# Two blocks on one core: experts' sums in pairs, the overflow loop inside a condition, and a ninth 2 MB slot for weights

## The chip, the cores and the metric

The kernel runs on one core of a Trainium2 chip. The time is the device time of one execution in microseconds (us). Of the core's engines, TensorE (PE in the profile) multiplies matrices, with weight loads (PEld) beside it; VectorE (DVE), ScalarE (ACT) and GpSimd (POOL) work on elements; SyncE (SP) only issues transfers from HBM, which 16 DMA engines carry out. SBUF is the memory on the chip, PSUM the memory into which TensorE writes.

## The reference

A token block of 256 x 1024 in float32 goes through two layers of a network. The first layer has a mixer, a layer norm and 32 experts of which each token takes 4; the second has another mixer and a gated MLP. The change lies in the first layer's norm and experts:

```python
h = layer_norm(DEEPNORM_ALPHA * h + mix, ln1_g[l], ln1_b[l])
ffn = moe(h, router_w[l], router_b[l], expert_w_up[l], expert_b_up[l], expert_w_down[l], expert_b_down[l])
h = layer_norm(DEEPNORM_ALPHA * h + ffn, ln2_g[l], ln2_b[l])

# moe, for each block of slots of one expert e:
hcat = xblk @ w_up[e] + b_up[e]                 # 1024 -> 2048
x_glu = minimum(hcat[:, 0::2], 7.0)
x_lin = clip(hcat[:, 1::2], -7.0, 7.0)
act = x_glu * sigmoid(1.702 * x_glu) * (x_lin + 1.0)
y = act @ w_down[e] + b_down[e]                 # 1024 -> 1024
# and for each token: the sum over its four experts of gate * y
```

One expert has 8.39 MB of up weights and 4.19 MB of down weights, 32 experts 402.7 MB, and each byte is read once. They come in chunks of 2.097 MB (2048 KB), called 2 MB here.

## The kernel before

The program is one long list of instructions for each engine, written out in Python; the order on each engine is the order of the code. It has three stages: the mixer of the first layer, the experts, and the second layer.

**Slots of an expert.** Each expert has 64 slots (`CAP`), to which the router's picks bring its tokens. `gather_group` (line 1079 issues its matmuls) brings the tokens of four experts at a time into `xt`, transposed, by matmuls with 0/1 matrices. An expert with more than 64 tokens puts the rest into an overflow table.

**One expert on TensorE.** `up` streams four chunks of 2 MB (two k-rows of 128 x 2048 each) and multiplies them with the expert's tokens (`up_k`, line 1027, 16 records a chunk), into `pu`. Inputs and outputs of 512 columns are laid as two halves of 64 partitions: 64 slots x two halves are 128 rows of PSUM. `swiglu` makes the activation on VectorE and ScalarE. `down` streams two chunks of 2 MB (`down_h`, line 1036, 16 records a chunk), and `out_copy` (line 1056) brings the result to SBUF as `y`, with columns 0 to 511 on partitions 0 to 63 and columns 512 to 1023 on partitions 64 to 127.

**Between the chunks.** The stages of several experts interlock. While expert e's up chunks run, behind the first of them, `between(1)` issues: the transposes of the activation of e-1 (`act_t`, line 1018), the sum of expert e-2's output into the tokens (`combine`, line 1066: four matmuls with 64 rows in, the gates at slots `gpt` as the stationary operand, and VectorE's addition of each to the tokens, line 1068), and the gates at slots for expert e (`gates_at_slots`: two picks on VectorE, line 1045, two transposes, line 1048, one copy). Then come the remaining three up chunks, and the down chunks of e-1. The last expert's down projection (`last_down`, lines 1161 and 1172) takes four pieces of 1 MB, so that the next norm's statistics can begin early. The last 2 MB chunk before the pieces is the second down chunk of expert 30.

**The ring of slots.** All weights come through `fetch` (line 129): it takes the oldest slot of a ring in SBUF and issues one transfer on SyncE's queue. A fetch into a slot waits until the engine that read it last is done. In the expert stage there are 8 slots of 2 MB: two in the arena `ring`, one in `ring1`, three in `ring2`, two in `lp`. They are filled ahead before the first expert starts, `lp` last, as its memory is in use until then.

**The middle.** After expert 15, and its two trailing sums, the number of overflow blocks is loaded into registers (line 1239), `lp` leaves the ring, six chunks are fetched ahead into the others, and a loop `For_i(0, n_over)` (line 1252) does the overflow blocks, with `lp` for their weights. Here the number is zero and the loop's body doesn't run; the loop's entry and exit synchronize all engines. Then `lp` joins the ring again, and experts 16 to 31 follow.

**The norm before the experts.** `route` normalizes the rows. Scale and shift (`ln1_g`, `ln1_b`) are folded into the weights of the router and the gathered tokens; for the residual path two rows are broadcast over 128 partitions by DMA, and GpSimd multiplies and adds them (`rest`). `gates` then scales by ALPHA and adds the gates times `b_down` (lines 931 and 933).

## Time and profile before

| | us |
|---|---|
| median of 3 runs (lowest, highest) | 1768.74 (1766.86, 1769.26) |
| the profiled execution | 1768.8 |
| its span, first to last instruction | 1767.0 |
| TensorE busy in it | 1656.0 (94%) |
| VectorE, ScalarE, GpSimd busy | 746.9, 556.8, 112.5 |
| bytes moved by DMA | 535.61 MB, 303 GB/s in the mean |
| mean granted clock of TensorE | 0.979 of full speed |

The profile is of one execution. Line numbers (L1027) are those of the program above. "Busy" of TensorE counts matmuls in the pipeline. Times in the views are counted from the start of the span. A group `pu<-ring,xt` says which tile is written and which are read. A wait is idle time of an engine just before an instruction, put down to what released it last. [...] The DMA share is the mean busy share of the 16 DMA engines; it can come out a little over 1.

### The profile page before, as it was taken

How to read it: one execution, taken by the hardware profiler on the slowest of the kernel's cores; microseconds unless marked ns; L12 is line 12 of the kernel's file. 1: busy time of each engine (PE TensorE's matmuls, PEld its weight loads, DVE VectorE, ACT ScalarE, POOL GpSimd, SP SyncE). 2: the span in 40 equal slices, each digit the busy share in tenths (PEclk: the TensorE clock that was granted, in tenths of full speed). 3: DMA queues.
4: the chain of work that ended last, by engine and by line, in shares of the span. 5: the costliest groups of instructions: out<-in, count | busy, mean ns of one | idle time of the engine just before them, and what ended most of it. 6: DMA issues, size and time to landing. Idle time of an engine off the chain costs nothing.

```text
span 1767.0 us, 23938 instructions
## 1 busy us (share of the span) xinstructions
PE 1656.0 (94%) x10141; PEld 1069.0 (60%) x10141; DVE 746.9 (42%) x1184; ACT 556.8 (32%) x859; POOL 112.5 (6%) x98
## 2 busy tenths in 40 slices
PE   8999989999999999799999999998999999999998
PEld 7999863333333333333333333347999999998997
DVE  5855542212222221122221222127677777566565
ACT  5446521110100100101001001015666556455444
POOL 5311220000000000000000000001211100000000
PEclk9999989999999999899999999998999999999999
DMA  9450979999999999899999999984554456455552
GB/s 314 134 165 1 351 287 427 404 407 427 427 427 427 426 428 427 359 418 427 427 428 428 426 428 427 427 313 157 174 168 139 148 168 207 164 167 191 191 187 76
DMA packets 149934, 535.61 MB, mean 303 GB/s; under 512 B 7123, under 2 KB 119139, under 8 KB 125504
## 3 DMA queue, kind: packets, MB, share of 16 engines
q1 hardware_dynamic: 147488, 529.68, 76.3%
q0 software_dynamic: 2048, 4.23, 0.8%
q8 instruction: 81, 1.33, 0.3%
q14 instruction: 29, 0.24, 0.0%
q10 hardware_dynamic: 288, 0.13, 0.0%
HBM read 532.97 MB, written 1.05 MB: 302 GB/s over the span
## 4 chain that ended last, share of the span: by engine, by line
PE 52%; DVE 4%; ACT 2%; issue 1%; DVEq 0%; ACTq 0%
PE pu L1027 13%; PE pj L163 8%; PE pj L165 7%; PE pj L164 7%; PE pd L1036 6%; PE pc L1066 2%; PE pa L164 1%; PE pa L163 1%; PE pa L165 1%; DVE xs L1068 1%; PE pc L1079 1%; DVE wl L158 1%; PE pu L1134 1%; PE px L1018 1%; PE po L1523 1%
## 5 line engine op out<-in xcount | busy, mean ns | idle before, releaser
L1027 PE MATMUL pu<-ring,xt 128*64 128x512 f32 x1600 | 369.2, 611 | 2.4 <-ACT xt L61 2.4
L158 DVE TENSOR_TENSOR wl<-ring,wh 128x1024 fp32r<-128x1024 f32 (+1 forms) x232 | 277.3, 1218 | 39.7 <-ACT wh L61 39.5
L61 ACT ACTIVATE wh<-ring 128x1024 fp32r<-128x1024 f32 (+1 forms) x247 | 252.3, 1029 | 85.8 <-PE pj L164 44.0
L1027 PEld LDWEIGHTS pu<-ring,xt 128*64 128x64 f32 x1600 | 111.5, 140 | 218.0 <-issue 209.7
L1068 DVE TENSOR_TENSOR xs<-xs,pc 128x512 f32<-128x512 f32 x124 | 79.7, 684 | 333.2 <-PE pc L1066 333.2
L1005 DVE TENSOR_SCALAR xg<-pu 128x512 f32<-128x512 f32 x32 | 22.1, 691 | 361.3 <-PE pu L1027 361.3
L165 PE MATMUL pj<-uth,wl 128*128 128x256 f32 x584 | 163.7, 280 | 4.4 <-DVE wl L158 4.4
L163 PE MATMUL pj<-uth,wh 128*128 128x256 f32 x584 | 165.7, 284 | 0.0
L164 PE MATMUL pj<-utl,wh 128*128 128x256 f32 x584 | 163.3, 280 | 0.0
L1036 PE MATMUL pd<-ring,act 128*64 128x512 f32 x704 | 154.8, 592 | 0.0
L61 ACT ACTIVATE sg<-xg 128x512 f32<-128x512 f32 x32 | 20.1, 630 | 334.9 <-DVE xg L1005 334.9
L165 PEld LDWEIGHTS pj<-uth,wl 128*128 128x128 f32 x584 | 110.5, 189 | 5.2 <-DVE wl L158 5.2
L163 PEld LDWEIGHTS pj<-uth,wh 128*128 128x128 f32 x584 | 110.8, 190 | 2.2 <-issue 2.1
L1066 PE MATMUL pc<-y,gpt 64*128 64x512 f32 x248 | 88.3, 641 | 24.9 <-DVE xs L1068 24.0
L1036 PEld LDWEIGHTS pd<-ring,act 128*64 128x64 f32 x704 | 50.5, 137 | 100.6 <-issue 100.6
L164 PEld LDWEIGHTS pj<-utl,wh 128*128 128x128 f32 x584 | 110.9, 190 | 0.1
L158 POOL TENSOR_TENSOR wl<-ring,wh 128x1024 fp32r<-128x1024 f32 x14 | 38.7, 2767 | 1093.2 <-PE pj L164 963.4
L1027 PE MATMUL pu<-lp,xt 128*64 128x512 f32 x448 | 104.2, 615 | 0.0
L163 PE MATMUL pj<-yah,wh 128*128 128x256 f32 x352 | 99.0, 281 | 0.0
L165 PE MATMUL pj<-yah,wl 128*128 128x256 f32 x352 | 98.9, 281 | 0.0
L164 PE MATMUL pj<-yal,wh 128*128 128x256 f32 x352 | 98.8, 281 | 0.0
L163 PE MATMUL pj<-xth,wh 128*128 128x256 f32 x288 | 83.1, 289 | 2.8 <-ACT wh L61 2.8
(441 smaller groups left out, 2808.6 us busy)
## 6 DMA issues: line engine op xcount, KB each, us to landing
ring<-in_expert_w_up_dram SPq DMA_DIRECT2D x100, 2048.0 KB, 18.8
ring<-in_expert_w_down_dram SPq DMA_DIRECT2D x44, 2048.0 KB, 16.4
ring<-in_w_in_dram SPq DMA_DIRECT2D x62, 1024.0 KB, 5.3
lp<-in_expert_w_up_dram SPq DMA_DIRECT2D x28, 2048.0 KB, 16.7
lp<-in_expert_w_down_dram SPq DMA_DIRECT2D x18, 2048.0 KB, 16.8
ring<-in_w_up_dram SPq DMA_DIRECT2D x22, 1024.0 KB, 5.0
ring<-in_w_down_dram SPq DMA_DIRECT2D x11, 1024.0 KB, 4.7
ring<-in_w_s_out_dram SPq DMA_DIRECT2D x8, 1024.0 KB, 4.8
```

Of the source, the lines that this page charges most:

```text
L61: self.nc.scalar.activation(out, x, func, **kw)
L158: return (hi_t, lo_t), lambda: (engine or g.nc.vector).tensor_sub(lo_t, src, hi_t)
L163: nc.tensor.matmul(out, a[0][asl], b[0][bsl], start=first, stop=False, skip_group_check=True)
L164: nc.tensor.matmul(out, a[0][asl], b[1][bsl], start=False, stop=False, skip_group_check=True)
L165: nc.tensor.matmul(out, a[1][asl], b[0][bsl], start=False, stop=last, skip_group_check=True)
L1005: nc.vector.tensor_scalar(xg, pv[:, :, 0], 7.0, None, op0=OP.min)
L1018: g.nc.tensor.transpose(pt[:, k], xv[:, k], g.ident)
L1027: g.nc.tensor.matmul(pu[hf * 64:hf * 64 + 64, b], x, ch[:, hf * D + b * 512:hf * D + b * 512 + 512], start=first, stop=last, skip_group_ch ...
L1036: g.nc.tensor.matmul(pd[n * 64:n * 64 + 64], act[:, k, hf], ch[:, s:s + 512], start=hf + k == 0, stop=hf * 4 + k == 7, skip_group_check=True)
L1066: nc.tensor.matmul(pc, gpt[s, tt], y[s], start=True, stop=True)
L1068: nc.vector.tensor_add(o, o, pc)
L1079: g.nc.tensor.matmul(pt[:, j], part[:, tt, (k + j) * P:(k + j + 1) * P], onehot(tt), start=tt + i == 0, stop=tt + i == 2)
```

## The change

- **A ninth slot.** The arena `ring2` gets 8 units instead of 6, so four slots of 2 MB instead of three; the ring of the expert stage has nine. Nine chunks are fetched before expert 0, and seven ahead of the loop. The memory comes from smaller scratch: the iota of 128 columns becomes one of 64, some tiles have one buffer instead of two, one tile of `swiglu` goes, and the scratch of GpSimd's DMA descriptors is 8192 instead of 16384 bytes.
- **Sums in pairs.** For an even expert e, `between(1)` issues the transposes alone; for an odd one it issues the sum of experts e-3 and e-2 together (`combine_pair`), and the gates at slots of experts e-1 and e (`pair_gates`). To put two experts' outputs on 128 partitions, `down` of an odd expert writes its column halves to the exchanged partitions, and two half copies on ScalarE lay the pair into one tile. Experts 30 and 31 are summed singly.
- **The condition.** The overflow loop stands inside `If(n_over > 0)`, and its loads are issued by GpSimd instead of SyncE.
- **Norm factors by products.** The broadcasts by DMA and GpSimd's four operations go. `gates`, now within experts 1 and 2, lets TensorE spread the scale over the partitions (eight matmuls with the identity), VectorE multiplies it into the tokens, and the shift comes in as a 33rd row of the product with `b_down`.
- **Swiglu.** The product with the sigmoid comes first, then the linear half.

```diff
@@ -36,7 +36,7 @@
 MANUAL = True
-RING, RING1, RING2 = 4, 2, 6
+RING, RING1, RING2 = 4, 2, 8
...
@@ -851,9 +852,7 @@
     n = len(g.ahead)
-    g.ahead += [fetch(g, *src) for src in (up_src(A, 0) + up_src(A, 1))[n:n + 2]]
-    ln = p.tile([P, 2, D], F32, name="ln")
-    gam, bet = bcast_row(g, ln[:, 0], "ln1_g"), bcast_row(g, ln[:, 1], "ln1_b")
+    g.ahead += [fetch(g, *src) for src in (up_src(A, 0) + up_src(A, 1) + down_src(A, 0))[n:n + 2]]
...
@@ -898,11 +897,7 @@
-    def rest():
-        for tt in range(2):
-            nc.gpsimd.tensor_mul(h[:, tt], h[:, tt], gam)
-            nc.gpsimd.tensor_add(h[:, tt], h[:, tt], bet)
-    return parts(), rest
+    return parts()
...
@@ -918,20 +913,31 @@
+    for n in range(2):
+        s = slice(n * 512, n * 512 + 512)
+        pt = pc_.tile([P, 512], F32, name="pc")
+        for k in range(4):
+            nc.tensor.matmul(pt[:, k * P:k * P + P], r.gb[:, 4 * n + k:4 * n + k + 1].to_broadcast([P, P]), g.ident,
+                             start=True, stop=True)
+        for tt in range(2):
+            nc.vector.scalar_tensor_tensor(h[:, tt, s], h[:, tt, s], ALPHA, pt, op0=OP.mult, op1=OP.mult)
+        yield
     pg = px.tile([NE, 2, P], F32, name="px")
     for tt in range(2):
         nc.tensor.transpose(pg[:, tt], r.gate[:, tt], g.ident)
-    nc.scalar.copy(gT, pg.rearrange("p a b -> p (a b)"))
+    nc.scalar.copy(gT[:NE], pg.rearrange("p a b -> p (a b)"))
     yield
     for tt in range(2):
         for n in range(2):
             pt = pc_.tile([P, 512], F32, name="pc")
             nc.tensor.matmul(pt, gT[:, tt * P:tt * P + P], r.bd[:, n * 512:n * 512 + 512], start=True, stop=True)
             s = slice(n * 512, n * 512 + 512)
-            nc.vector.scalar_tensor_tensor(h[:, tt, s], h[:, tt, s], ALPHA, pt, op0=OP.mult, op1=OP.add)
-    yield
+            nc.vector.tensor_add(h[:, tt, s], h[:, tt, s], pt)
+        yield
...
@@ -1000,13 +1006,12 @@
     xg = wp.tile([P, 512], F32, name="xg", bufs=1)
-    xl = wp.tile([P, 512], F32, name="xl", bufs=1)
     sg = wp.tile([P, 512], F32, name="sg", bufs=1)
     nc.vector.tensor_scalar(xg, pv[:, :, 0], 7.0, None, op0=OP.min)
     g.act(sg, xg, AF.Sigmoid, scale=1.702)
-    nc.vector.tensor_scalar(xl, pv[:, :, 1], 7.0, -7.0, op0=OP.min, op1=OP.max)
-    nc.vector.scalar_tensor_tensor(xg, xl, 1.0, xg, op0=OP.add, op1=OP.mult)
     nc.vector.tensor_mul(xg, xg, sg)
+    nc.vector.tensor_scalar(sg, pv[:, :, 1], 7.0, -7.0, op0=OP.min, op1=OP.max)
+    nc.vector.scalar_tensor_tensor(xg, sg, 1.0, xg, op0=OP.add, op1=OP.mult)
...
@@ -1028,26 +1033,52 @@
-def down_h(g, pd, act, ch, hf):
+def down_h(g, pd, act, ch, hf, swap=0):
     for k in range(4):
         for n in range(2):
             s = k * D + n * 512
-            g.nc.tensor.matmul(pd[n * 64:n * 64 + 64], act[:, k, hf], ch[:, s:s + 512],
+            m = (n ^ swap) * 64
+            g.nc.tensor.matmul(pd[m:m + 64], act[:, k, hf], ch[:, s:s + 512],
                                start=hf + k == 0, stop=hf * 4 + k == 7, skip_group_check=True)
...
@@ -1028,26 +1033,52 @@
+def pair_gates(g, r, wp, px, e, both=True):
+
+
+    nc = g.nc
+    gp = wp.tile([P, 2, 4, CAP], F32, name="gp", bufs=1)
+    for tt in range(2):
+        for i in range(2):
+            at = (slice(0, 3, 2) if i == 0 else slice(1, 2)) if both else slice(2 * i, 2 * i + 2)
+            n = 1 if both and i else 2
+            nc.vector.tensor_scalar(gp[:, tt, at], r.iota[:, None, :].to_broadcast([P, n, CAP]),
+                                    r.pos[:, tt, e + i:e + i + 1], r.gate[:, tt, e + i:e + i + 1],
+                                    op0=OP.is_equal, op1=OP.mult)
+    pt = px.tile([P, 2, 2, P], F32, name="px")
+    for i in range(2):
+        a = i if both else 2 * i
+        for tt in range(2):
+            nc.tensor.transpose(pt[:, i, tt], gp[:, tt, a:a + 2].rearrange("p a s -> p (a s)"), g.ident)
+    gpt = wp.tile([P, 2, 2, P], F32, name="gpt", bufs=1)
+    nc.scalar.copy(gpt.rearrange("p i t s -> p (i t s)"), pt.rearrange("p i t s -> p (i t s)"))
     return gpt
...
@@ -1064,6 +1095,17 @@
+def combine_pair(g, acc, pc_, y, gpt):
+
+    nc = g.nc
+    for tt in range(2):
+        for n in range(2):
+            pc = pc_.tile([P, 512], F32, name="pc")
+            nc.tensor.matmul(pc, gpt[:, n, tt], y[:, n], start=True, stop=True)
             o = acc[:, tt, n * 512:n * 512 + 512]
             nc.vector.tensor_add(o, o, pc)
...
@@ -1146,7 +1188,7 @@
         def at_slots(e):
-            gpt[e] = gates_at_slots(g, r, wp, px, lambda tt: r.pos[:, tt, e:e + 1], lambda tt: r.gate[:, tt, e:e + 1])
+            gpt[e] = pair_gates(g, r, wp, px, e, e < NE - 2)
...
@@ -1179,8 +1221,15 @@
             for hf, src in enumerate(down_src(A, e)):
-                down_h(g, pd, act[e], stream(g, *src), hf)
-            y[e] = out_copy(g, wp, pd)
+                down_h(g, pd, act[e], stream(g, *src), hf, e % 2)
+            if e == NE - 2:
+                y[e] = out_copy(g, wp, pd)
+                return
+            if e % 2 == 0:
+                y[e] = wp.tile([P, 2, 512], F32, name="y", bufs=1)
+            for i in range(2):
+                s = slice(i * 64, i * 64 + 64)
+                nc.scalar.copy(y[e - e % 2][s, i ^ (e % 2)], pd[s])
...
@@ -1190,27 +1239,24 @@
                 next(parts)
-                rest()
             for e in range(e0, e1 + 2):
                 def between(k, e=e):
                     if e == e0 and k in (0, 2, 4):
                         next(first)
                     if e == e0 and k == 5:
                         picks(e + 1)
-                    if e == 2 and k in begin:
-                        begin[k]()
+                    for f in begin.get((e, k), ()):
+                        f()
                     if k != 1:
                         return
                     if e0 < e <= e1:
                         act[e - 1] = act_t(g, wp, px, act[e - 1], e == NE)
-                    if e == 2:
-                        return
-                    if e > e0 + 1 and e - 2 in y:
-                        combine(g, acc, pc_, y.pop(e - 2), gpt.pop(e - 2))
-                    if e == 3:
-                        at_slots(2)
-                    if 2 < e < e1:
-                        at_slots(e)
+                    if e == NE:
+                        combine(g, acc, pc_, y.pop(e - 2), gpt[e - 2][:, 0])
+                    if e % 2 == 1 and e - 3 in y:
+                        combine_pair(g, acc, pc_, y.pop(e - 3), gpt.pop(e - 3))
+                    if e % 2 == 1 and 2 < e < e1:
+                        at_slots(e - 1)
...
@@ -1227,19 +1273,20 @@
+        step = lambda: next(gt)
+        begin = {(1, 5): [step], (1, 6): [step], (1, 7): [step], (2, 0): [step], (2, 2): [step], (2, 3): [step],
+                 (2, 5): [lambda: at_slots(0)]}
...
@@ -1227,19 +1273,20 @@
         drop_ring(g, lp)
         g.ahead = [fetch(g, *src) for src in (up_src(A, half) + up_src(A, half + 1))[:len(g.slots)]]
-        overflow(g, acc, n_over, lp, wp, pu_, px, pd_, pc_)
+        with tc.If(n_over > 0):
+            overflow(g, acc, n_over, lp, wp, pu_, px, pd_, pc_)
...
@@ -1940,7 +1987,7 @@
-    nc = bacc.Bacc("TRN2", target_bir_lowering=False, num_devices=1)
+    nc = bacc.Bacc("TRN2", target_bir_lowering=False, num_devices=1, dynamic_dma_scratch_size=8192)
```

SyncE's order at the start of the experts, from the first fetch of expert weights (`ring1`, `ring`, `ring2` and `lp` are the arenas; the numbers tell tiles of one name apart). Before:

```order
L129 DMA ring_84<-in_w_out_dram 128x8x256
L129 DMA ring1_94<-in_expert_w_up_dram 128x4096
L129 DMA ring_84<-in_expert_w_up_dram 128x4096
L129 DMA ring2_1983<-in_expert_w_up_dram 128x4096 x3
L129 DMA ring_84<-in_expert_w_up_dram 128x4096
L129 DMA lp_2578<-in_expert_w_up_dram 128x4096 x2
L129 DMA ring1_94<-in_expert_w_down_dram 128x4096
```

and now:

```order
L129 DMA ring1_94<-in_expert_w_up_dram 128x4096
L129 DMA ring_84<-in_expert_w_up_dram 128x4096 x2
L129 DMA ring2_1983<-in_expert_w_up_dram 128x4096 x4
L129 DMA lp_2579<-in_expert_w_up_dram 128x4096
L129 DMA lp_2579<-in_expert_w_down_dram 128x4096
L129 DMA ring1_94<-in_expert_w_down_dram 128x4096
L129 DMA ring_84<-in_expert_w_up_dram 128x4096 x2
L129 DMA ring2_1983<-in_expert_w_up_dram 128x4096 x2
```

Before, eight fetches stand ahead of the one into `ring1` that follows on the use of chunk 0; now there are nine, the last a down chunk of expert 0.

SyncE's order in the middle, around the loop. Before (the loop's body is left out):

```order
L129 DMA ring2_1983<-in_expert_w_up_dram 128x4096 x3
L129 DMA ring_84<-in_expert_w_up_dram 128x4096
L1252 COMPARE_AND_BRANCH
L1252 UNCONDITIONAL_BRANCH x2
...
L1252 REGISTER_ALU
L1252 COMPARE_AND_BRANCH
L1252 UNCONDITIONAL_BRANCH
L129 DMA lp_2578<-in_expert_w_up_dram 128x4096 x2
```

and now:

```order
L129 DMA ring1_94<-in_expert_w_up_dram 128x4096
L129 DMA ring_84<-in_expert_w_up_dram 128x4096 x2
L129 DMA ring2_1983<-in_expert_w_up_dram 128x4096 x3
L1288 COMPARE_AND_BRANCH
L1299 COMPARE_AND_BRANCH
L1299 UNCONDITIONAL_BRANCH x2
L1998 BRANCH_PREFETCH_HINT
L1299 REGISTER_ALU
L1299 COMPARE_AND_BRANCH
L1299 UNCONDITIONAL_BRANCH
L1288 UNCONDITIONAL_BRANCH
L129 DMA lp_2579<-in_expert_w_up_dram 128x4096
```

Seven fetches instead of six stand ahead of the loop, and the branch of line 1288 passes over all that belongs to the loop (line 1299); its body has no transfer on SyncE any more.

TensorE's order over one expert before, in the first half (line 1134 is the bias that opens `pu`, 1027 up, 1018 the transposes of the activation, 1066 the sum, 1048 the gates at slots, 1036 down):

```order
L1134 MATMUL pu<-bup,pick 128x512 x2
L1027 MATMUL pu<-ring_1983,xt 64x512 x8
L1018 MATMUL px<-ident,xg 128x128 x4
L1066 MATMUL pc<-y,gpt 128x512 x4
L1048 MATMUL px<-ident,gp 128x128 x2
L1027 MATMUL pu<-ring_1983,xt 64x512 x16
L1027 MATMUL pu<-ring,xt 64x512 x8
L1036 MATMUL pd<-lp,act 64x512 x16
```

and over an even expert and the beginning of an odd one now (1176 bias, 1032 up, 1023 transposes, 1042 down, 1108 the sum of a pair, 1079 the gates of a pair):

```order
L1176 MATMUL pu<-bup,pick 128x512 x2
L1032 MATMUL pu<-ring_1983,xt 64x512 x8
L1023 MATMUL px<-ident,xg 128x128 x4
L1032 MATMUL pu<-ring_1983,xt 64x512 x16
L1032 MATMUL pu<-lp,xt 64x512 x8
L1042 MATMUL pd<-lp,act 64x512 x8
L1042 MATMUL pd<-ring_94,act 64x512 x8
L1176 MATMUL pu<-bup,pick 128x512 x2
L1032 MATMUL pu<-ring,xt 64x512 x8
L1023 MATMUL px<-ident,xg 128x128 x4
L1108 MATMUL pc<-y,gpt 128x512 x4
L1079 MATMUL px<-ident,gp 128x128 x4
```

The four matmuls of the sum stood in each expert and stand in every second one; the transposes for the gates are four in every second expert instead of two in each.

## Rows read from the trace of the kernel before

**Rows 1.** Windows: start:end, length, busy time (count) by engine, granted clock, DMA share, GB/s.

```profile
240.00:1190.00 950.00, 878.35 (x3974) 324.42 (x3974) 212.46 (x421) 112.82 (x205) 9.50 (x5) 0.97 0.99 414
...
400.00:700.00 300.00, 280.63 (x1251) 101.29 (x1249) 65.05 (x131) 30.24 (x57) 0.00 (x0) 0.98 1.01 427
```

**Rows 2.** TensorE's waits, 300 to 1250: releaser, total us, times, longest us.

```profile
PE px L1048 <- DVE gp L1045: 30.5, 27, 1.1
PE pc L1066 <- DVE xs L1068: 24.0, 31, 0.8
PE pu L1134 <- SPq L1252: 8.1, 1, 8.1
```

**Rows 3.** SyncE queue's waits, 205 to 1250: releaser, total us, times, longest us.

```profile
SPq L129 <- PE pu L1027: 643.3, 125, 16.7
SPq L129 <- PE pd L1036: 172.6, 58, 3.0
```

**Rows 4.** DMA issues by tile and source: count, KB each, median us to landing.

```profile
ring<-in_expert_w_up_dram SPq DMA_DIRECT2D x100, 2048.0 KB, 18.8
...
ring<-in_w_s_out_dram SPq DMA_DIRECT2D x8, 1024.0 KB, 4.8
```

**Rows 5.** SyncE timeline before the experts: start us, length us, issues, count.

```profile
192.87 34.96 SPq L129 DMA_DIRECT2D ring<-in_expert_w_up_dram  x6
239.67 1.08 SPq L129 DMA_DIRECT2D lp<-in_expert_w_up_dram  x2
255.21 6.40 SPq L129 DMA_DIRECT2D ring<-in_expert_w_down_dram  x2
```

**Rows 6.** TensorE timeline, expert 0: start us, length us, instructions, count, [idle before].

```profile
248.03 3.68 PE L1027 MATMUL pu<-ring,xt 128*64 128x512 f32 x8 [0.66 <-ACT xt L61]
...
253.23 1.94 PE L1027 MATMUL pu<-ring,xt 128*64 128x512 f32 x8
```

**Rows 7.** Windows at the first weights and where the DMA falls idle.

```profile
242.50:252.50 10.00, 8.71 (x25) 4.55 (x26) 5.46 (x10) 4.24 (x5) 0.00 (x0) 0.50 0.88 368
250.00:260.00 10.00, 8.88 (x41) 3.81 (x40) 4.61 (x8) 3.78 (x6) 2.90 (x2) 0.87 0.49 180
340.00:350.00 10.00, 10.00 (x46) 3.28 (x44) 0.29 (x1) 0.00 (x0) 0.00 (x0) 0.93 0.81 326
...
720.00:730.00 10.00, 1.91 (x6) 0.68 (x4) 2.22 (x5) 0.00 (x0) 0.00 (x0) 0.69 0.51 215
484.80:488.20 3.40, 3.40 (x14) 1.40 (x15) 0.85 (x2) 0.37 (x1) 0.00 (x0) 0.50 1.03 439
```

**Rows 8.** TensorE groups, 300 to 1190: count, busy us, mean ns, idle before.

```profile
L1027 PE MATMUL pu<-ring,xt 128*64 128x512 f32 x1476 | 338.8, 610 | 0.7 <-ACT xt L61 0.7
...
L1066 PE MATMUL pc<-y,gpt 64*128 64x512 f32 x248 | 88.3, 641 | 24.9 <-DVE xs L1068 24.0 <-ACT y L1056 0.7
...
L1018 PE MATMUL px<-ident,xg 128*128 128x128 f32 x120 | 22.5, 310 | 0.0
```

**Rows 9.** TensorE timeline at the loop.

```profile
728.89 1.22 PE L1134 MATMUL pu<-bup,pick 128*128 128x512 f32 x2 [8.09 <-SPq L1252]
```

**Rows 10.** The loop's own instructions (line 1252): shortest/median/longest ns, first and last start.

```profile
L1252 PEldq COMPARE_BRANCH  x3: 97/192/5961, 720.4 to 728.6; - x3
```

**Rows 11.** SyncE timeline around the loop.

```profile
691.37 14.06 SPq L129 DMA_DIRECT2D ring<-in_expert_w_up_dram  x5
729.58 0.81 SPq L129 DMA_DIRECT2D lp<-in_expert_w_up_dram  x2
```

**Rows 12.** TensorE timeline at the end of the experts.

```profile
1169.38 7.04 PE L1036 MATMUL pd<-ring,act 128*64 128x512 f32 x32
...
1180.71 1.97 PE L1161 MATMUL pu<-lp,act 128*64 128x128 f32 x32
```

**Rows 13.** VectorE's gate picks (line 1045): count, shortest/median/longest ns.

```profile
L1045 DVE TENSOR_SCALAR gp<-io,pos,gate x64: 337/341/347, 305.7 to 1158.4; 128x128 f32<-128x128 f32 x64
```

## The prediction

> **What bounds the kernel now.** I read the windows first, because the share of busy time of the whole run mixes three stages. The experts take 950 of the 1767 us of the span [rows 1], and in that stage both TensorE and the DMA engines look full: TensorE 878 us busy, the DMA share 0.99. So the next view is who waits. TensorE's waits from 300 to 1250 us name VectorE and once the loop, but not one DMA [rows 2]: every weight chunk was there before it was wanted. SyncE's queue, which issues the chunks, waited for TensorE 183 times, 816 us together [rows 3]. So TensorE sets the pace, and a slot that it frees is filled at once. The third view is how far behind the DMA is, and here lies the case: from 400 to 700 us the share is 1.01 at 427 GB/s [rows 1], and an issue lands 18.8 us later in the median [rows 4], where 2048 KB by itself take 2.097 MB / 427 GB/s = 4.91 us. There are always about four chunks in the queue. The DMA engines have nothing left to give, TensorE is only a little slower than they are. What TensorE gains is worth something only until it meets the weights.

> **Two clocks.** So I work out two ends of the expert stage and take the later one. The mark for both is the last whole 2 MB chunk, the second half of the down projection of expert 30 (chunk 189, counted from 0: 32 experts x 6 chunks, less the two that come as four 1 MB pieces). Before, TensorE came to it in the middle of its group of 32 records: 1169.38 + 7.04 / 2 = 1172.9 us [rows 12]. From there to the end the program is the same in both, and moves as a whole.

> *TensorE's own clock.* It takes up chunk 0 at 248.0 [rows 6], so 924.9 us lie before the mark. The edits, one by one:
> - Sums in pairs. A combine of one expert is 8 records of line 1066: (88.3 + 24.9) / 31 = 3.65 us with its wait for VectorE [rows 8]. A pair has the same 8 records, with 128 rows in where there were 64. No row shows this with both widths; the records of 128 rows on this engine (line 1027) take 610 ns and those of 64 rows 641 [rows 8], so I take the same 3.65 (bounds: none to 1.0 us more for each pair). 31 combines become 16: 15 x 3.65 = 54.8 us less (40 to 55).
> - Gates at slots. Four picks for a pair in one go instead of two for each expert, 341 ns each [rows 13]. TensorE waited 30.5 / 27 = 1.13 us each time [rows 2], 0.45 us beyond two picks; for a pair I take 4 x 0.34 + 0.45 = 1.8, so 15 x (2.26 - 1.8) = 7 us less (0 to 15).
> - Norm factors by products: 8 matmuls more, at the 310 ns of line 1018 [rows 8] 2.5 us on TensorE (0 to 5). The two broadcasts and four GpSimd operations that go had no waiter in rows 2.
> - Swiglu in another order: VectorE now waits for the sigmoid, some 0.7 us later. The down projection before the transposes need it takes 7.04 us [rows 12], so it costs nothing; bare it would be 32 x 0.7 = 22 us.
> - The condition: TensorE's branch of 5.96 us stays [rows 10], what goes is the barrier around it, at most 8.09 - 5.96 = 2.1 us [rows 9].
> - Halves of the down output swapped, two half copies on ScalarE: under the next expert's first chunk, nothing on TensorE.
> Sum: 924.9 - 54.8 - 7 - 2.1 + 2.5 = 863.5, and TensorE by itself would be at the mark at 248.0 + 863.5 = 1111.5 us.

> *The weights' clock.* Six chunks are issued by 227.8 and two at 239.7 [rows 5]; then the DMA falls idle (share 0.49 from 250 to 260 [rows 7]), since all eight slots are full until TensorE frees chunk 0 at 255.21. The ninth slot is filled in the idle time before 239.7, so nine chunks lie there at about 239.7 + 2.2 + 2 x 4.91 = 251.7. The 2.2 us are the landing of a lone 1 MB transfer, 4.8 us, less its 2.46 us at 427 GB/s [rows 4]. The tenth chunk (9) is still issued at 255.2. From it to chunk 189 are 181 chunks: 181 x 4.911 = 888.9, and the last lands at 255.2 + 888.9 + 2.2 = 1146.3, if the DMA never stops again. The two places where it stopped before: at 340 to 350 (share 0.81, 1.9 us [rows 7]; the ninth slot is 4.91 us of room there) and at the loop, where SyncE stood from 705 to 729.6 [rows 11] and the share of 720 to 730 is 0.51 [rows 7]. Now SyncE passes the condition by a branch without a barrier. Seven chunks are in the queue then, 34 us, against some 20 us until TensorE is past its own branch and the first slot behind it can be filled. So I add 0 to 5 us, taking 1, for the first experts alone.

> 1146.3 is 35 us later than 1111.5: the weights decide. TensorE is behind them at first (nine chunks) and gains 4.911 - 863.5 / 190 = 0.37 us at each chunk, so the waits should begin near chunk 80, about 640 us, and sum to some 35 us. The mark: 1146.3 + 1 (a stop) + 1 (from landing to the matmul, and part of a chunk at half clock) = 1148.3, 24.6 us earlier than 1172.9. The four last pieces are 9.8 us of transfer, TensorE wants the first 7.8 us behind the mark (1180.71 [rows 12]) and the rest as they come, so they are covered. **The profiled execution's 1768.8 us (span 1767.0; it lies within 0.1 us of the median) less 24.6 gives 1744.2 us.**

> So of some 61 us taken from TensorE about 25 arrive. The ninth slot and the condition without a barrier are what keep the DMA from stopping; with the pairs alone it would stop as before near 255 and at the loop.

> **Half clock.** From 242.5 to 252.5 the granted clock is 0.50, and eight records of line 1027 take 3.68 us, at full clock 1.94 [rows 6, 7]. Later it falls again for single stretches of 3.4 us (484.8 to 488.2: 0.50 [rows 7]), with TensorE busy throughout and no DMA waited for. [...]

> **Rivals.**
> - TensorE stays the bound, because the pairs save little (a pair of full width takes up to 6 us, or the longer odd expert breaks the stride). For it: the row of 64 against 128 rows doesn't isolate the width. Against: 35 us of margin. It needs 35 us back out of 61, and then each further us counts; at 45 us back the gain is about 15: 1754. Up to 1765 if nearly all is lost. 8%.
> - Early stops. TensorE runs its slowest in experts 0 to 4 (routing tables, gates, half clock), and the ring is full in just that time. Every us that the DMA stops is lost for good, as it has no reserve. With 5 to 9 us of stops: 1748 to 1752. For it: the stop of 1.9 us at 340 to 350 [rows 7], with eight slots. 20%.
> [...]
> - The change doesn't do what it says: the loop's barrier remains in another form, or the ninth slot comes too late, and the DMA stops for about 5 us at each place as before (shares 0.49 and 0.51 of 10 us [rows 7]): 1754. 6%.
> - Better: the first chunk at full clock (255.2 becomes 251.5) or the stretch from landing to use at nothing: 1739 to 1742. 7%.

> **Chances.** The forecast (1742 to 1748) has 55%, the rivals 8, 20, 4, 6 and 7. A difference under 0.2% (3.5 us) can't be told from none here. Same is the far end of the first rival, 3%; slower is the clock with a little for the unforeseen, 5%; faster 92%. The range 1740 to 1755 leaves out some 15 to 20%: the better case's end, the loss of nearly all, the slower case.

> **What will show it.** Right: TensorE's waits name the DMA in the later experts, some 30 to 40 us, beginning between 500 and 750 us; windows of 100 us from 260 to 1140 all at 427 GB/s, that around the loop too; line 1066's successor at 128 records plus the single one, 3.6 us for a pair; the mark near 1148. Wrong: no wait for a DMA in the experts (TensorE still bounds), a DMA share under 0.97 in a window, a pair well over 4 us, or a granted clock under 0.95 for the stage.

## The result and the profile after

The changed kernel takes 1746.76 us (median of 4 runs, 1743.83 to 1747.61) against 1769.0 us before (4 runs of the same series): ratio 0.9873, interval 0.9857 to 0.989. Two later series on the same kernel gave 0.9879 (0.9861 to 0.9897) and 0.9879 (0.9858 to 0.9899). The forecast was 1744.2 us, 24.6 us less; measured are 22.2 us less. The profiled execution has a span of 1746.0 us, 21.0 less than before.

The windows answer to [rows 1, 7] (columns as there):

```profile
240.00:1170.00 930.00, 845.67 (x3870) 310.78 (x3870) 183.88 (x366) 127.26 (x219) 0.00 (x0) 0.99 1.00 421
250.00:260.00 10.00, 8.46 (x42) 3.46 (x40) 4.76 (x8) 3.64 (x5) 0.00 (x0) 0.91 0.51 177
340.00:350.00 10.00, 10.00 (x49) 3.17 (x45) 3.37 (x5) 0.63 (x1) 0.00 (x0) 1.00 1.01 428
400.00:700.00 300.00, 276.35 (x1231) 99.09 (x1228) 58.16 (x117) 37.39 (x66) 0.00 (x0) 0.99 1.01 427
720.00:730.00 10.00, 9.27 (x45) 3.53 (x46) 3.36 (x9) 1.80 (x3) 0.00 (x0) 1.00 1.01 428
```

The experts' stage is full of transfers (share 1.00). The windows at 340 and at 720, where the DMA engines had fallen idle, are full too; only the stop at 250 to 260 is left. TensorE's granted clock for the stage (the share of its full speed that it was allowed, 1.00 or 0.50 in the trace's records of it) rose from 0.97 to 0.99. TensorE's waits, before without one DMA [rows 2]:

```profile
PE pd L1042 <- DMA ring<-in_expert_w_down_dram: 25.2, 26, 2.4
PE px L1079 <- DVE gp L1072: 18.7, 14, 1.4
PE pu L1032 <- DMA ring<-in_expert_w_up_dram: 17.1, 20, 1.3
...
PE pu L1032 <- DMA lp<-in_expert_w_up_dram: 5.6, 8, 1.2
...
PE pd L1042 <- DMA lp<-in_expert_w_down_dram: 1.3, 1, 1.3
```

Now 55 waits for weights with 49.2 us lead the list; by the same view up to 620 us they are 4.1 us, the rest comes later. None of them is longer than 2.4 us. The wait of the sum for VectorE, 24.0 us before, is not in the list any more. The groups of TensorE for the sums and the gates (against 88.3 + 24.9 us and 30.5 us of waits, [rows 8, 2]):

```profile
L1108 PE MATMUL pc<-y,gpt 128*128 128x512 f32 x120 | 56.9, 607 | 1.3 <-ACTq L1288 1.3
...
L1079 PE MATMUL px<-ident,gp 128*128 128x128 f32 x64 | 13.2, 293 | 20.7 <-DVE gp L1072 18.7 <-ACT act L1025 0.7
```

15 pairs in 56.9 us are 3.79 us for a pair. One expert before took 88.3 / 31 = 2.85 us of work and 24.9 / 31 = 0.80 us of wait. SyncE at the start, against [rows 5]:

```profile
192.51 35.42 SPq L129 DMA_DIRECT2D ring<-in_expert_w_up_dram  x7
239.76 0.33 SPq L129 DMA_DIRECT2D lp<-in_expert_w_up_dram  x1
240.13 0.43 SPq L129 DMA_DIRECT2D lp<-in_expert_w_down_dram  x1
254.96 0.33 SPq L129 DMA_DIRECT2D ring<-in_expert_w_down_dram  x1
```

Seven chunks and two go out ahead, and the tenth follows at 254.96, as before. TensorE's branch in the middle, against 5961 ns [rows 10]:

```profile
L1288 PEldq COMPARE_BRANCH  x1: 352/352/352, 697.3 to 697.3; - x1
```

Last, the chain of waits at the end of the experts (start, length, what; a DMA piece runs from its issue to its landing):

```profile
1074.69 38.82 DMA ring<-in_expert_w_up_dram
...
1113.57 39.22 DMA ring<-in_expert_w_down_dram
...
1152.84 3.68 PE pd L1042 x16
```

The chain hangs on transfers: 1074.69 + 38.82 is the landing of one chunk, 0.06 us later the last one is issued, 39.22 us later that lands, and TensorE starts 0.05 us after. 39.2 us are eight chunks of 4.90: here SyncE issues a chunk when the eighth before it has landed (0.06 us after it for this one), so that eight are on their way and no more, although there are nine slots. SyncE's own waits (205 to 1250 us, as [rows 3]) name a transfer of weights 109 times, with 399.7 us in all; before, one such wait of 3.0 us stands in the list. The largest group of them:

```profile
SPq L129 <- DMA ring<-in_expert_w_up_dram: 211.1, 54, 9.4
```

The mark of the prediction, the second down chunk of expert 30, is at 1152.84 (forecast 1148.3, before 1172.9): 20.1 of the 21.0 us of the span are gained up to there.

### The profile page after: what moved, and what is told of

Its sections match the earlier page's. It is cut to its first block, busy times and chain, and to the rows that moved or that the text cites. A ratio compares the mean times of both kernels' runs of the same rounds, so it can differ in the third digit from the quotient of the medians.

```text
span 1746.0 us, 23590 instructions
## 1 busy us (share of the span) xinstructions
PE 1620.8 (93%) x10037; PEld 1052.8 (60%) x10037; DVE 718.8 (41%) x1129; ACT 571.2 (33%) x873; POOL 101.9 (6%) x93
## 4 chain that ended last, share of the span: by engine, by line
PE 37%; DMA 18%; DVE 3%; ACT 1%; issue 1%; DVEq 0%; ACTq 0%; SPq 0%
DMA ring<-in_expert_w_up_dram 11%; PE pj L163 8%; PE pj L165 8%; PE pj L164 7%; PE pu L1032 6%; DMA lp<-in_expert_w_up_dram 4%; DMA ring<-in_expert_w_down_dram 2%; PE pa L164 1%; PE pa L165 1%; PE pa L163 1%; PE pc L1108 1%; DVE wl L158 1%; PE po L1570 1%; PE pu L1203 0%; PE po L360 0%
## 5 line engine op out<-in xcount | busy, mean ns | idle before, releaser
L1032 PE MATMUL pu<-ring,xt 128*64 128x512 f32 x1568 | 353.4, 599 | 20.1 <-DMA ring<-in_expert_w_up_dram 17.1
L1032 PEld LDWEIGHTS pu<-ring,xt 128*64 128x64 f32 x1568 | 107.1, 137 | 232.4 <-issue 195.0
L1042 PE MATMUL pd<-ring,act 128*64 128x512 f32 x832 | 189.2, 600 | 26.5 <-DMA ring<-in_expert_w_down_dram 25.2
L1042 PEld LDWEIGHTS pd<-ring,act 128*64 128x64 f32 x832 | 59.4, 138 | 152.6 <-issue 115.6
L61 ACT ACTIVATE sg<-xg 128x512 f32<-128x512 f32 x32 | 20.1, 629 | 340.6 <-DVE xg L1010 340.6
L1032 PE MATMUL pu<-lp,xt 128*64 128x512 f32 x480 | 110.9, 604 | 5.6 <-DMA lp<-in_expert_w_up_dram 5.6
L1232 ACT COPY y<-pd 64x512 f32<-64x512 f32 x60 | 34.8, 580 | 202.2 <-PE pd L1042 201.8
L1110 DVE TENSOR_TENSOR xs<-xs,pc 128x512 f32<-128x512 f32 x60 | 41.3, 688 | 107.7 <-PE pc L1108 107.7
```

The source lines that it names most:

```text
L61: self.nc.scalar.activation(out, x, func, **kw)
L1032: g.nc.tensor.matmul(pu[hf * 64:hf * 64 + 64, b], x, ch[:, hf * D + b * 512:hf * D + b * 512 + 512], start=first, stop=last, skip_group_ch ...
L1042: g.nc.tensor.matmul(pd[m:m + 64], act[:, k, hf], ch[:, s:s + 512], start=hf + k == 0, stop=hf * 4 + k == 7, skip_group_check=True)
L1110: nc.vector.tensor_add(o, o, pc)
L1232: nc.scalar.copy(y[e - e % 2][s, i ^ (e % 2)], pd[s])
```

## The experiments

The theory that the result left (A): from the middle of the experts on the transfers bound the kernel, and a chunk has landed when the slowest of 16 DMA engines has done its part. Rivals stand in each expectation. Single runs stray by 3 to 5 us around their median, and not only by the experts: with eight slots the profiled execution began the second block 5 us later and yet had the span of the run beside it (1746.3 and 1745.9). So I read the mark beside the time. Ratios are to the kernel before, on the same chip.

**The changed kernel again**, as the measure for the others.

> The changed kernel as it is, as the measure for the three beside it. Theory A (the weights' transfers bound the experts from about the middle on, and a chunk counts as landed when the slowest of the 16 DMA engines has done its part): 1746 to 1748 us, and the DMA waits of TensorE again 45 to 52 us.

1747.49 us (5 runs), ratio 0.9879, mark at 1153.52, waits for DMA 51.3 us.

**Eight slots.**

```diff
-RING, RING1, RING2 = 4, 2, 8
+RING, RING1, RING2 = 4, 2, 6
```

> The changed kernel with eight slots instead of nine. Theory A: one chunk less lies ready when expert 0 starts, and the weights' clock has no reserve, so the whole 4.9 us come back: 1751 to 1752.5 us; the waits for DMA grow by the same. Rival (the ring is full in the slow first experts, so that the ninth slot was worth more than one chunk): 1754 to 1757. Rival (TensorE's clock decides): no change, 1746 to 1748.

1754.2 us (6 runs, 1747.86 to 1757.39), ratio 0.9919 (0.9902 to 0.9936); the mark is at 1158.46, 4.94 us later than in the run beside it. That is the one chunk of 4.91 us: the ninth slot is worth its place in the start and no more, which fits the chain above with its eight transfers on their way. The medians differ by 6.7 us, with runs that spread over 9.5 us. By the median that is the first rival's range (1754 to 1757); the mark speaks for theory A.

**The loop without the condition.**

```diff
-        with tc.If(n_over > 0):
-            overflow(g, acc, n_over, lp, wp, pu_, px, pd_, pc_)
+        overflow(g, acc, n_over, lp, wp, pu_, px, pd_, pc_)
```

> The changed kernel with the overflow loop bare, as before the change, so that SyncE stands at the loop until all engines have passed it. The prediction's term: the DMA runs dry there, about 5 us more, 1751 to 1753 us. Theory A: TensorE now reaches the loop right behind the weights, with seven chunks or 34 us still in the queue, and SyncE stands for some 10 to 20 us only; the DMA doesn't run dry, 1746 to 1748 us, and the window around the loop stays at 426 to 428 GB/s.

1749.77 us (6 runs), ratio 0.9895 (0.9878 to 0.9912), mark at 1155.86: 2.3 us later, between the two expected. SyncE's issues, its waits at the loop (line 1298 here), and the window:

```profile
671.87 21.01 SPq L129 DMA_DIRECT2D ring<-in_expert_w_up_dram  x6
723.70 0.33 SPq L129 DMA_DIRECT2D lp<-in_expert_w_up_dram  x1
```

```profile
SPq L1298 <- DMA ring<-in_expert_w_up_dram: 29.5, 3, 19.9
```

```profile
715.00:725.00 10.00, 0.81 (x2) 0.72 (x3) 0.69 (x1) 0.00 (x0) 0.00 (x0) 0.50 0.66 261
```

I had it that SyncE would stand there for 10 to 20 us and the queue would outlast it. That was wrong: at the loop's entry, as the program is built, SyncE waited 29.5 us for transfers to land, the queue ran dry, and nothing was issued until 723.70. The share of 0.66 instead of 1.01 over 10 us is a stop of 3.5 us in the mean of the DMA engines, where the prediction had about 5. The mark moved by 2.3 only. The trace has sixteen landing events for each transfer, which I take as one of each DMA engine, and these show why. On the engine that is done first the last whole chunk landed at 1152.1, 5.5 us later than in the run beside it (1146.6); on the engine that is done last it landed only 2.3 us later (1155.8 and 1153.5). The parts of a chunk had come to lie 3.9 us apart before the stop. Behind it all engines began anew together, 0.4 us apart, and at the end they were 3.7 us apart, where the run beside it has 6.9.

TensorE stood at the loop as well:

```profile
PE pu L1176 <- issue: 26.5, 1, 26.5
```

It made up most of that, since seven chunks lay ready when it went on: its waits for weights are 32.3 us in this run and 51.3 in the run beside it.

**Single sums**, with nine slots and the condition (`gates_at_slots`, `combine` and `out_copy` for each expert, as in the kernel before).

> The changed kernel with nine slots and the condition, but each expert's output summed by itself, as before the change. Theory A: TensorE has its 54.8 + 7 us again and decides once more, since its clock then ends some 27 us behind the weights': 1762 to 1768 us, and hardly a wait for DMA in the experts. Rival (a good part of the gain came from the DMA never stopping, by the ninth slot and the condition, and the pairs are only one way to more of it): 1750 to 1757.

1763.46 us (12 runs), ratio 0.998 (0.9966 to 0.9993). TensorE's waits again hold no DMA, and the old ones are back:

```profile
PE px L1057 <- DVE gp L1052: 30.5, 27, 1.1
PE pc L1097 <- DVE xs L1099: 24.0, 31, 0.8
```

The pairs are what brings the gain; all the rest of the change (slot, condition, norm factors, swiglu) brings 0.2% without them.

**No sums of pairs** (the outputs of experts 0 to 29 are not added).

```diff
-                        combine_pair(g, acc, pc_, y.pop(e - 3), gpt.pop(e - 3))
+                        y.pop(e - 3), gpt.pop(e - 3)
```

> The changed kernel without the 15 sums of pairs (the outputs of experts 0 to 29 are not added to the tokens): 15 x 3.65 = 55 us less on TensorE. Theory A: TensorE only waits longer, 1745 to 1748 us, with 95 to 105 us of waits for DMA. Rival (TensorE bounds in a part of the stage, as where the clock falls or in the first experts): each expert in that part gives 1.8 us, 1720 to 1740 us.

1748.55 us (6 runs), ratio 0.9884 (0.9864 to 0.9904), 0.6 us above what theory A had: no gain from 55 us less work on TensorE. The waits for DMA:

```profile
PE pd L1042 <- DMA ring<-in_expert_w_down_dram: 46.4, 39, 1.3
PE pu L1032 <- DMA ring<-in_expert_w_up_dram: 39.2, 44, 2.0
...
PE pu L1032 <- DMA lp<-in_expert_w_up_dram: 10.9, 13, 1.3
PE pd L1042 <- DMA lp<-in_expert_w_down_dram: 9.2, 7, 1.5
```

Together 105.7 us against 51.3 in the run beside it: the whole difference has become waiting. This settles that the weights bound the stage. The granted clock of TensorE stays up under these waits:

```profile
760.00:1090.00 330.00, 273.80 (x1258) 96.44 (x1258) 40.95 (x83) 41.38 (x74) 0.00 (x0) 1.00 1.01 427
```

**Five chunks for each expert**, so that TensorE shows its own clock (the second half of the down projection uses the first chunk's weights).

```diff
-                down_h(g, pd, act[e], stream(g, *src), hf, e % 2)
+                if hf == 0 or g.ahead:
+                    ch = stream(g, *src)
+                down_h(g, pd, act[e], ch, hf, e % 2)
```

> The changed kernel in which the second down chunk of experts 0 to 30 is not fetched (the first chunk's weights are used for it too): TensorE has the same work, the DMA 31 chunks or 152 us less. This shows TensorE's own clock. The prediction's sum (its mark at 1111.5 us): 41 us less than the changed kernel, 1705 to 1707. By the waits measured in the changed kernel (49 us for DMA in the experts): 1697 to 1699.

1682.68 us (5 runs), ratio 0.9528 (0.9507 to 0.9548), further down than either figure. TensorE's waits name no DMA in this run, so it runs by its own clock. Its timeline at the mark, and its window:

```profile
1087.51 7.04 PE L1042 MATMUL pd<-ring,act 128*64 128x512 f32 x32
```

```profile
250.00:1090.00 840.00, 811.84 (x3679) 297.69 (x3677) 170.95 (x332) 121.79 (x210) 0.00 (x0) 1.00 0.93 383
```

The mark is at 1087.51 + 3.52 = 1091.0, where the prediction's sum had 1111.5; that sum was 20 us too high, and the reserve against the weights some 60 us instead of 35.

**More code on GpSimd.** The landing events show that the DMA engines drift apart in steps. From 250 to 1150 us the queues that carry the engines' code had 30 packets of 16 KB (1.07 us each in the mean) and 8 of 8 KB (0.32 us). I take the lags of the sixteen parts of a chunk behind the first part, and add them up. In the last run of the changed kernel 16 of the 16 KB packets stand apart from the others: from the second chunk before such a packet to the third behind it the sum rises by 1.60 us in the mean (1.50 to 1.70). In 13 stretches of three chunks without a packet it moves by some 0.2 us at most.

```diff
+            for _ in range(160):
+                nc.gpsimd.memset(idle, 0.0)
             pd = pd_.tile([P, 512], F32, name="pd")
...
+        idle = p.tile([P, 1], F32, name="idle")
```

> The changed kernel with 160 tiny memsets on GpSimd, idle otherwise in this stage, ahead of each of 31 down projections: 4960 instructions more, which no other engine waits for. Theory (the 16 DMA engines drift apart because every 16 KB of code that an engine fetches is one packet that holds up one of them by about a microsecond, and a chunk has landed only when the last of them is done): some 20 packets or more on the queue of instructions beside the 80 now, the spread of the last chunk's landing grows from 7 us to 8.5 to 11, and the mark and the time come 1.5 to 4 us later, 1748.5 to 1751.5. Rival (the drift comes from the memory, not from the code): spread 6.5 to 7.5, time 1746 to 1748.

1764.18 us (12 runs), ratio 0.9986 (0.9973 to 0.9999): some 17 us above the changed kernel on the other chips, 19 by the ratios, far more than expected. With half the memsets:

> The changed kernel with 80 instead of 160 tiny memsets on GpSimd for each of 31 experts. With 160 the packets on GpSimd's queue of instructions went from 28 to 67, and one single DMA engine landed 25 us after the first, the other fifteen as ever within 6.5. Theory (GpSimd's code is brought by one DMA engine, 0.64 us a packet): some 47 packets, that engine 12 to 13 us behind at the last chunk, the others as before, and the time 5 to 7 us above the changed kernel. Rival (the memsets delay in another way, as by GpSimd's use of the memory's ports): the delay doesn't follow one engine, or isn't about half.

1755.95 us (6 runs), ratio 0.9926 (0.9909 to 0.9942); the changed kernel beside it 1747.32. The time is 8.6 us later, more than the 5 to 7 expected; the mark is 5.9 us later. The queues of instructions (packets, MB, share) of the changed kernel:

```profile
q8 instruction: 80, 1.31, 0.3%
q14 instruction: 28, 0.23, 0.0%
```

with 80 memsets:

```profile
q14 instruction: 47, 0.39, 0.1%
```

with 160:

```profile
q14 instruction: 67, 0.54, 0.1%
```

The 4960 memsets are 39 packets of 8 KB, which is 64 bytes for each. By the landings they all fall to one DMA engine: at the last whole chunk it landed 25.1 us after the first with 160 memsets and 12.7 us after with 80, while the other fifteen lay within 6.5 and 7.1 us. That is 25.1 / 39 = 0.64 us for a packet, twice the 0.32 us that such a packet itself took; why twice is open. With 80 memsets the additional packets came up to 628 us, and the engine's lag, 12.8 us at 666, stayed at that to the end. The marks follow: 1152.84 without memsets, 1158.77 with 80 and 1172.30 with 160. The chain with 160 memsets:

```profile
1133.13 39.13 DMA ring<-in_expert_w_down_dram
...
1172.30 3.68 PE pd L1042 x16
```

GpSimd did nothing that anyone waited for; its code cost some 17 us, as one sixteenth of each chunk landed late, at the last whole chunk by those 25.1 us. So the code brought to an engine set the DMA engines apart here. The size expected was wrong: I had spread the packets over all engines. The drift of some 7 us in the changed kernel fits the code that it has anyway: from 288 to 1145 us the sum of the lags grows from 7.9 to 58.5 us, by 50.6, and 29 packets of 16 KB and 7 of 8 KB make 29 x 1.60 + 7 x 0.64 = 50.9. That is read from the trace alone, as no run took that code away.

**Halves at the start.**

```diff
-    g.nc.sync.dma_start(v, src)
+    g.turns = getattr(g, 'turns', 0) + (size == WIDE)
+    if 10 <= g.turns <= 14:
+        g.nc.sync.dma_start(v[:, :SLOT], src[:, :SLOT])
+        g.nc.sync.dma_start(v[:, SLOT:], src[:, SLOT:])
+    else:
+        g.nc.sync.dma_start(v, src)
```

Turns 10 to 14 are the fetches after the first nine.

> The changed kernel with the five fetches after the first nine issued as two halves of 1 MB each, so that a half slot is filled again as soon as TensorE has used it. The DMA's stop near 252 to 256 us then ends when the first half of chunk 0 is used, about 252, instead of 255, and chunk 1's halves are worth 2.5 us too: the weights' clock, which decides, comes 2 to 3 us earlier, 1743.5 to 1745.5. Rival (the stop isn't on the path, or the halves cost as much): 1746 to 1748.

1746.05 us (6 runs), ratio 0.9885 (0.9867 to 0.9904). SyncE's first issues, the window, and the mark:

```profile
251.83 0.33 SPq L131 DMA_DIRECT2D ring<-in_expert_w_down_dram  x1
254.85 0.33 SPq L132 DMA_DIRECT2D ring<-in_expert_w_down_dram  x1
```

```profile
250.00:260.00 10.00, 8.38 (x42) 3.46 (x40) 4.74 (x8) 3.66 (x5) 0.00 (x0) 0.92 0.76 265
```

```profile
1150.77 3.65 PE L1047 MATMUL pd<-ring,act 128*64 128x512 f32 x16 [0.58 <-DMA ring<-in_expert_w_down_dram]
```

The stop shrinks (share 0.76 instead of 0.51) and the mark comes 2.1 to 2.8 us earlier than in the two runs of the changed kernel above, as expected. The time doesn't show it: 1746.05 us lies in the rival's range, and its ratio can't be told from those of the changed kernel.

**More halves.**

```diff
-    g.nc.sync.dma_start(v, src)
+    g.turns = getattr(g, 'turns', 0) + (size == WIDE and n == size)
+    if size == WIDE and n == size and (10 <= g.turns <= 14 or 187 <= g.turns <= 190):
+        g.nc.sync.dma_start(v[:, :SLOT], src[:, :SLOT])
+        g.nc.sync.dma_start(v[:, SLOT:], src[:, SLOT:])
+    else:
+        g.nc.sync.dma_start(v, src)
...
-                    if e == e0 and k in (0, 2, 4):
+                    if e == e0 and k in (1, 3, 5):
                         next(first)
```

> The changed kernel with the five fetches after the first nine and the last four whole chunks issued as halves of 1 MB, and the gathers of the first expert of each half moved behind the odd k-rows, so that chunk 0 is used up earlier. Theory A (the weights bound, so every us that the DMA starts earlier, and every us that TensorE needs less after the last landing, is one of the time): the start gives 2 to 3 us, as the marks of the half fetches alone showed, the gathers up to 1 more, and half a chunk less after the last landing 1.8: 4 to 6 us in all, a ratio to the changed kernel of 0.9965 to 0.998. Rival (halves only shift the wait, as the drift of the DMA engines grows by as much): within 2 us of the changed kernel.

> The changed kernel once more, as the measure for the two beside it: ratio to the kernel before 0.986 to 0.989, and the second down chunk of expert 30 begun between 1152 and 1154.5 us.

1746.95 us (4 runs), ratio 0.9878 (0.9858 to 0.9898), and the changed kernel beside it 1747.32, 0.9879, mark at 1152.84. The gain isn't there. The start was lost to the moved gathers: TensorE now waits for the gathered tokens `xt` at each chunk of expert 0.

```profile
262.61 3.65 PE L1037 MATMUL pu<-ring,xt 128*64 128x512 f32 x16 [0.66 <-ACT xt L61]
268.06 3.65 PE L1037 MATMUL pu<-ring,xt 128*64 128x512 f32 x16 [0.66 <-ACT xt L61]
271.64 0.73 PE L1181 MATMUL pu<-bup,pick 128*128 128x512 f32 x2
```

With the halves at the start alone TensorE was through expert 0's chunks earlier:

```profile
269.47 0.74 PE L1181 MATMUL pu<-bup,pick 128*128 128x512 f32 x2
```

Of these 2.2 us this execution was 0.7 behind from the start on. Its last 2 MB chunk was there at 1153.7; with the halves at the start alone it was there at 1150.7, in the changed kernel beside it at 1152.8. So the transfers gained nothing here, and halves at the end were not tried on a start that had gained. They had little to give:

```profile
1138.91 3.65 PE L1037 MATMUL pu<-lp,xt 128*64 128x512 f32 x16
1142.40 7.04 PE L1037 MATMUL pu<-ring,xt 128*64 128x512 f32 x32
1149.27 7.04 PE L1047 MATMUL pd<-ring,act 128*64 128x512 f32 x32
```

No wait for weights stands here; with whole chunks the only one in this stretch is the 0.58 us in front of the mark (last line shown for the run before). TensorE is done with expert 30 at 1156.3, as in the changed kernel (1152.84 + 3.65 = 1156.5). No version here is shown to beat the changed kernel.

## Why the prediction was right, and where not

The mechanism was right: two clocks, the later one decides, and it is the weights' (without the sums no gain, with five chunks a ratio of 0.9528). Point by point:

- **Sums in pairs**: 3.65 us forecast for a pair, 3.79 measured, and 16 sums instead of 31. The sum is right; that the price is so near is in part luck, as the work on a pair grew from 2.85 to 3.79 us and the wait for VectorE of 0.80 us went. Without the pairs the gain is gone (single sums).
- **Gates at slots**: waits of 18.7 us over 14 or 1.34 us a pair, forecast 1.8. The waits fell by 30.5 - 18.7 = 11.8 us, forecast 7 (0 to 15).
- **Norm factors and swiglu** were not tried by themselves. With single sums, which keep them beside slot and condition, the mark is at 1172.6, before at 1172.8: no cost shows.
- **TensorE's own clock**, 1111.5 forecast, 1091.0 measured, so 20.5 us too high. The branch of 5.96 us was said to stay; it took 0.35 us here (though 5.7 us again with single sums, and why it comes and goes is open). The gates gave 4.8 us more than forecast, the sums 3.5 us less (51.3 of 54.8). And the granted clock rose, which no term had: by the trace's records of it TensorE worked at half clock for 40 us of the way to the mark before and for 7 us with five chunks, which is 16 us of time. These four make 23 us, so the split is a rough one. With single sums the granted clock from 640 to 760 is 0.94, before 0.93, in the changed kernel 1.00: it rose with the pairs, by what is open. It changed nothing, as this clock doesn't decide.
- **The weights' clock** is the term that was mis-sized: "the last lands at 255.2 + 888.9 + 2.2 = 1146.3" (2.2 should be 4.8 - 2.46 = 2.3). The first of the 16 DMA engines landed it at 1145.3, near what the mean rate gives; the last at 1152.8. It counted when its last sixteenth was there: TensorE began on it at 1152.84. In the kernel before that spread was 6.1 us at this chunk and cost nothing, since even its last part landed 3.0 us before TensorE began on it (1169.8 and 1172.8); 427 GB/s as a mean over a stretch can't show it.
- **The gain** came within 2.4 us of the forecast in part by luck. The landing is 6.5 us later than the sum has it. Two allowances of 1 us each took up 2 of these, though neither was needed: in the windows from 258 to 1090 the DMA share is 1.00 or 1.01, and TensorE starts 0.05 us after the landing. Another 0.9 us was gained behind the mark, and 1.2 us lie between the profiled execution (21.0 us less) and the medians (22.2).
- **The ninth slot**: one chunk, 4.94 us at the mark, right.
- **The condition**: the stop that it removes is there, 3.5 us by the window (forecast about 5), but the reason given was half of it. At the bare loop SyncE waited 29.5 us for its transfers to land, not only until TensorE had passed. At the mark the condition is worth 2.3 us, as the stop set the engines even again (0.4 us apart behind it).
- **The waits**: forecast some 35 us from about 640 us on; 49.2 us, of which 45.1 after 620.
- **Slower, by the clock** (the third of the five chances of the rivals, 4%): that waits for weights bring TensorE's granted clock down was my assumption, which no run showed beforehand. The 55 waits for weights, 0.9 us in the mean or a quarter of a chunk's 3.65 us, left the granted clock of the stage at 0.99, above the 0.97 of before, and 103 such waits without the sums left it at 1.00 from 760 to 1090. One stretch at half clock does follow a wait, the longest: 2.4 us, over at 1059.9, and half clock from 1060.8 to 1064.3. The last run of the changed kernel, with no wait for weights over 1.3 us, has none there.
- **The other rivals**: "TensorE stays the bound" is refuted by the run without sums, "early stops" and "the change doesn't do what it says" by the full windows at 340 and 720.

## What to carry to other kernels

Work out the end of a stage for each resource apart and take the latest: it told that of 61 us (81, as it turned out) taken from TensorE only about 25 would arrive; 22 did. With transfers as the bound, the slowest DMA engine set the time here (1152.8 us), not the mean rate (1146.3 by the prediction's sum), so leave the spread of landings in the sum. And code was traffic here: 4960 more instructions on GpSimd, which had nothing else to do, cost some 17 us by the DMA engine that also carried a part of the weights.
